# A one-core decoder trunk: last output piece of 128 columns instead of 256, and the first block's norm-weight product queued behind the third block's high part

## The chip, the cores and the metric

The kernel runs on one core of a Trainium2 chip. A core has TensorE (matrix products, PE in the profile), VectorE (DVE), ScalarE (ACT), GpSimd (POOL) and SyncE (SP). Each runs its own instructions in a fixed order, and they wait for one another through semaphores. SyncE, ScalarE and GpSimd also issue DMAs, which move data between the chip's main memory and the on-chip memory; the queue of the issuing engine is written SPq or ACTq. Products are gathered in PSUM, banks of 512 float32 per partition. The metric is the device time of one execution in microseconds (us). Three runs of the kernel before took 1330.47 to 1331.39 us, with a median of 1330.71 us.

## The reference

One layer of a decoder trunk on 1024 tokens with 1024 channels, in float32:

```python
xn = rmsnorm(x, norm_mix_w[l])
proj = xn @ w_in[l]
...
y_da = diff_attention(da_q, da_k, da_v, lam, lam_init, subln_w[l])
y_sw = sliding_window_attention(sw_q, sw_k, sw_v, sinks[l])
merged = jax.nn.sigmoid(g_da) * (y_da @ w_br_da[l]) + jax.nn.sigmoid(g_sw) * (y_sw @ w_br_sw[l])
x = x + merged @ w_mix_out[l]
xn = rmsnorm(x, norm_ffn_w[l])
x = x + conv_ffn(xn, w_up[l], conv_w[l], conv_b[l], w_down[l])
...
return rmsnorm(x, norm_final_w)
```

`rmsnorm` multiplies by 1/sqrt(mean of squares + eps) and by a weight per channel. Two places matter here: the input norm's weight with the first product, `xn @ w_in`, and the product with `w_down` with the final norm behind it.

## The kernel before

Everything is kept transposed: channels lie on the 128 partitions, in 8 blocks of 128 channels, and the 1024 tokens lie along the columns, in two halves of 512. Each float32 operand is split into a high part, rounded to the type that the profile calls fp32r, and a low part, the rest; a product is then three matmuls (high by high, high by low, low by high). In most of the products a scheme after Strassen and Winograd replaces eight block products by seven, at the price of sums and differences of blocks on VectorE and GpSimd.

The order in which each engine gets its instructions is worked out when the kernel is built: a planner simulates the engines and lets the instruction that is ready go first, by program order among the ready ones. `tc.issue_after(ins)` forbids part of that: what is written inside the block for the engine of `ins` is queued behind `ins`. It adds no wait for `ins` to finish, and other engines' instructions inside the block, such as a DMA issued by SyncE, are not held.

**The front** (`project`, L278 to L436). The blocks of x are loaded in the order 0, 4, 1, 5, 2, 6, 3, 7 (`rows`), the first two in halves. For each block `cut` (L348) writes the high part xh on ScalarE (L351, x times the norm weight, rounded) and the low part xl on VectorE (L352). `blocks` (L299) then issues the matmuls of this block for the three column blocks of `w_in` that are computed in the plain way (L304 to L306). Those weights come in pieces: the first block's, then three blocks' worth (`piece(n, 1, 4)`, L339 on ScalarE and L340 on VectorE). For the later products x itself is needed in differences: `scale(0)` (L370, L372) multiplies the blocks 0 and 4 by the norm weight on ScalarE, in place, `diffs(0)` (L312 to L315) makes four half differences on VectorE, and `parts(0)` (L838, L839) splits them. Only then are the buffers of the blocks 0 and 4 free for the blocks 3 and 7, since there are six. `square` (L364 to L368) collects the squares for the norm itself, which is applied after the product (L421, L429).

**The end** (`down`, L1078, and `last_norm`, L1234). The seven block products of `w_down` run as stages, the last of them "P4". Its four products m = 0 to 3 finish the first half's channel blocks 4 to 7. For m = 0 and 1 a product is 24 matmuls of 512 columns (L1169 in `product`). For m = 2 and 3 the 512 columns are cut into two pieces at `q` (L1093, 256 columns): first both products of columns 0 to 255, then both of columns 256 to 511. Behind each product come the eviction (L1223 on VectorE, x plus the PSUM sum), the square (L1158 on ScalarE), the sum of squares (L1160 on VectorE, not for the last channel block) and the product with the final norm's weight (L1161 on ScalarE).

`last_norm` gives back a list of steps for one piece of columns. `sums` adds the squares over the partitions with matmuls against ones (L185, one instruction stands twice for each block of 128 columns and operand), takes the mean on VectorE (L192) and the power -1/2 on GpSimd (L194). `spread` brings the result to all partitions with transposes (L200), twice, into two PSUM tiles, and copies the second one into the on-chip memory on ScalarE (L1251), because GpSimd's products read it there. Then come the scaled products of a few channel blocks each (L1259, on VectorE or GpSimd) with an output DMA for each (L1260), on SyncE and ScalarE in turn. For pieces shorter than 512 columns, `spread` and all products form one step. `tail` holds the steps that are still to be called: while the second piece's products are issued, `each` calls the first piece's steps, `sums` after the fifth k of m = 2 and the rest after the third k of m = 3. The second piece's steps are called behind everything.

## Time and profile before

| what | before |
|---|---|
| median of 3 runs | 1330.71 us |
| the profiled execution | 1330.42 us |
| its span, first to last instruction | 1328.4 us |
| granted TensorE clock, mean | 0.998 |
| VectorE, ScalarE, GpSimd busy | 1049.4, 614.7, 478.0 us |

The profiled execution lies 0.3 us below the median, and its span leaves out 2.0 us around the first and the last instruction. A row of the timeline has the start in us, the duration in us, the engine, the line, the operation, the tile written and those read, the shape, and how many such instructions follow one another (x2); in square brackets stands how long the engine was idle before and what released it. A row of the chain of waits has start, length and place of one link. A group's row has the busy time in us and the mean duration of one in ns. A row of the table by windows has the stretch, its length, the busy time and number of instructions of PE, PE's weight loads, DVE, ACT and POOL, the granted clock, the busy share of the DMA engines and GB/s. A row of the DMA issues has the queue, the count, the KB of one and the us from issue to landing.

### The profile page before, as it was taken

What the parts mean: (1) busy time and instruction counts of PE and PEld (TensorE: products, weight loads), DVE (VectorE), ACT (ScalarE), POOL (GpSimd) and SP (SyncE); (2) the same over time, 40 slices, a digit from 0 to 9 for tenths busy, and PEclk for the clock granted to TensorE, in tenths of its full rate; (3) what the DMA queues carried; (4) which work ended last, traced back from release to release, by engine and by line L of the source; (5) the groups of instructions that cost most, each with busy time, mean ns of one, the idle gap of its engine ahead of it and who ended that gap; (6) DMA issues with size and microseconds to landing.
All of it is one profiled execution on the core that took longest, in us unless ns stands there. A gap on an engine that the chain in (4) does not pass through costs nothing.

```text
span 1328.4 us, 17040 instructions
## 1 busy us (share of the span) xinstructions
PE 1315.8 (99%) x6264; PEld 1097.6 (83%) x6264; DVE 1049.4 (79%) x1431; ACT 614.7 (46%) x946; POOL 478.0 (36%) x364
## 2 busy tenths in 40 slices
PE   9999999999999999999999999999999999999997
PEld 7888888888888878888888888888888888888886
DVE  8846775289888976455669999999999997886654
ACT  9432232276667774333444443343434344345643
POOL 0446652001101015751435666665566631101111
PEclk9999999999999999999999999999999999999999
DMA  7334333966554236334422222122222228867532
GB/s 260 126 144 157 145 148 122 269 179 190 143 133 142 82 126 225 120 118 151 143 95 95 80 79 93 66 95 80 82 77 86 81 75 333 266 158 143 111 98 108
DMA packets 63234, 180.25 MB, mean 136 GB/s; under 512 B 6960, under 2 KB 16816, under 8 KB 63152
## 3 DMA queue, kind: packets, MB, share of 16 engines
q1 hardware_dynamic: 49120, 153.48, 35.1%
q0 software_dynamic: 2304, 8.39, 3.7%
q10 hardware_dynamic: 11728, 17.31, 3.6%
q8 instruction: 49, 0.80, 0.3%
q14 instruction: 33, 0.27, 0.1%
HBM read 130.39 MB, written 48.76 MB: 135 GB/s over the span
## 4 chain that ended last, share of the span: by engine, by line
PE 97%; ACT 1%; DVE 1%; DMA 0%; issue 0%; SPq 0%; POOLq 0%; POOL 0%; ACTq 0%
PE t L919 45%; PE y L1169 7%; PE d L1169 5%; PE g L177 4%; PE g L178 4%; PE g L179 4%; PE sc L177 3%; PE sc L179 3%; PE sc L178 3%; PE sc L651 3%; PE y L1120 2%; PE d L1120 2%; PE t L667 1%; PE t L770 1%; PE sc L739 1%; PE t L679 1%
## 5 line engine op out<-in xcount | busy, mean ns | idle before, releaser
L1063 POOL TENSOR_TENSOR us<-us,rstd 128x1024 f32<-128x1024 f32 x42 | 92.2, 2214 | 82.5 <-DVE us L484 47.6
L1072 ACT ACTIVATE c<-us,vecs 128x1024 f32<-128x1024 f32 x44 | 54.8, 1248 | 127.1 <-POOL us L1063 121.5
L137 DVE TENSOR_TENSOR sl<-sf,sh 128x1024 fp32r<-128x1024 f32 x62 | 89.3, 1441 | 12.8 <-ACT sh L135 12.8
L158 DVE TENSOR_TENSOR wl<-raw,wh 128x1024 fp32r<-128x1024 f32 (+1 forms) x49 | 68.0, 1389 | 35.5 <-ACT wh L156 25.9
L135 ACT CAST sh<-sf 128x1024 fp32r<-128x1024 f32 x62 | 64.6, 1044 | 62.1 <-PE t L919 44.0
L156 ACT CAST wh<-raw 128x1024 fp32r<-128x1024 f32 (+1 forms) x49 | 49.6, 1014 | 91.2 <-PE sc L178 33.4
L121 POOL TENSOR_TENSOR sf<-rv 128x512 f32<-128x512 f32 x30 | 50.4, 1679 | 99.5 <-DVE sl L137 59.0
L1169 PE MATMUL y<-h,wh 128*128 128x512 f32 (+1 forms) x288 | 80.8, 366 | 0.0
L1075 DVE SCALAR_TENSOR_TENSOR c<-us,vecs,c 128x1024 f32<-128x1024 f32 x44 | 78.5, 1817 | 0.0
L1074 DVE SCALAR_TENSOR_TENSOR c<-us,vecs,c 128x1024 f32<-128x1024 f32 x44 | 69.3, 1606 | 5.6 <-ACT c L1072 5.5
L123 POOL TENSOR_TENSOR sf<-raw,rv 128x512 f32<-128x512 f32 x30 | 56.7, 1890 | 46.6 <-DVE sl L137 46.6
L177 PE MATMUL g<-xh,wh 128*128 128x512 f32 x176 | 71.0, 404 | 1.5 <-ACT g L580 1.5
L178 PE MATMUL g<-xl,wh 128*128 128x512 f32 x176 | 70.3, 400 | 0.0
L179 PE MATMUL g<-xh,wl 128*128 128x512 f32 x176 | 70.2, 399 | 0.0
L1055 ACT ACTIVATE c<-c 128x1024 f32<-128x1024 f32 x22 | 23.4, 1063 | 83.4 <-DVE c L1075 83.4
L655 DVE CUSTOM_DVE_ANT_0 L<-sc,bias 128x128 f32<-128x128 f32 (+7 forms) x64 | 47.7, 752 | 17.0 <-PE sc L651 13.7
L634 POOL MEMSET aT<- 128x128 f32 x32 | 6.1, 204 | 151.8 <-PE t L680 98.0
L137 DVE TENSOR_TENSOR wl<-raw,wh 128x1024 fp32r<-128x1024 f32 (+1 forms) x32 | 59.7, 1864 | 0.1
L1169 PE MATMUL d<-h,wh 128*128 128x512 f32 x192 | 59.4, 390 | 0.0
L1169 PEld LDWEIGHTS y<-h,wh 128*128 128x128 f32 x288 | 52.1, 189 | 8.7
L122 POOL TENSOR_TENSOR sf<-sf,raw 128x512 f32<-128x512 f32 x31 | 58.2, 1878 | 2.2
L656 ACT ACTIVATE L<-L,sm 128x128 f32<-128x128 f32 (+7 forms) x64 | 49.6, 778 | 20.0 <-DVE sm L655 17.3
(411 smaller groups left out, 4255.4 us busy)
## 6 DMA issues: line engine op xcount, KB each, us to landing
u<-qd SPq DMA_DIRECT2D x72, 256.0 KB, 6.4
raw<-in_w_up SPq DMA_DIRECT2D x23, 512.0 KB, 3.5
raw<-in_w_in SPq DMA_DIRECT2D x22, 512.0 KB, 3.7
hd<-c SPq DMA_DIRECT2D x22, 512.0 KB, 2.6
rv<-in_w_up SPq DMA_DIRECT2D x21, 512.0 KB, 3.6
gr<-gd SPq DMA_DIRECT2D x16, 512.0 KB, 3.4
S<-in_w_down POOLq DMA_DIRECT2D x16, 512.0 KB, 6.7
qd<-us SPq DMA_DIRECT2D x15, 512.0 KB, 2.6
```

Of the source, the lines that this page charges most:

```text
L122: tt(sa[:, 1], sa[:, 0], g[:, 0], ALU.subtract)
L135: cast = nc.scalar.copy(hi, src)
L137: low = nc.vector.tensor_tensor(lo, src, hi.bitcast(F32), ALU.subtract)
L158: self.lo = (eng or nc.vector).tensor_tensor(wl, raw, wh.bitcast(F32), ALU.subtract)
L177: nc.tensor.matmul(ps, wh[:, kc + o, :], ah, start=first and n == 0, stop=False)
L178: nc.tensor.matmul(ps, wh[:, kc + o, :], al, start=False, stop=False)
L179: nc.tensor.matmul(ps, wl[:, kc + o, :], ah, start=False, stop=last and n == len(kcs) - 1)
L919: nc.tensor.matmul(ps, (ah, ah, al)[p][:, k, :], (bh, bl, bh)[p], start=first and n == p == 0, stop=last and p == 2 and n == len(ks) - 1, ...
L1063: i = (nc.vector if m % NF == 0 else nc.gpsimd).tensor_tensor(us[:, 2:], us[:, 2:], self.rstd, ALU.mult)
L1074: nc.vector.scalar_tensor_tensor(c, us[:, 1:T + 1], cw[1], c, ALU.mult, ALU.add)
L1075: nc.vector.scalar_tensor_tensor(c, us[:, 0:T], cw[0], c, ALU.mult, ALU.add)
L1169: nc.tensor.matmul(ps, v[:, k, :], x, start=start and k == i == 0, stop=k == 7 and i == 2, skip_group_check=True)
```

## The change

It has two parts.

At the front `cut` keeps its ScalarE instruction, and `third` is the one of the third block loaded, block 1. Both instructions of `scale(0)` are queued behind it on ScalarE.

At the end `q` becomes 384: the first piece has 384 columns, the last 128. The first piece's steps are now separate ones for all pieces: `sums` is called after the last k of m = 2 of the last piece, and three steps after the sixth k of m = 3: `spread`, the GpSimd product of channel blocks 6 and 7, and the VectorE product of blocks 0 and 1. The other two VectorE products, of blocks 2 and 3 and of blocks 4 and 5, are called among the last piece's own steps, the one ahead of its `sums`, the other ahead of its `spread`; on VectorE they are queued behind `ev`, the last eviction. The last piece's products are now of the channel blocks 0 to 2 (VectorE), 5 to 7 (GpSimd) and 3 and 4 (VectorE), three where there were four.

```diff
-                    nc.scalar.mul(self.xh[kc][:, a:b], x, wcol(kc))
+                    self.cut = nc.scalar.mul(self.xh[kc][:, a:b], x, wcol(kc))
...
                 for kc in rows[2:6]:
                     load(kc)
+                    if kc == rows[2]:
+                        third = self.cut.ins
                 nc.sync.dma_start(self.vecs[:, KC:], self.vecs_d[:, KC:])
                 for kc in rows[:2]:
                     square(kc)
-                scale(0)
+                with tc.issue_after(third):
+                    scale(0)
                 diffs(0)
...
-            q = H2 // 2
+            q = 3 * P
...
-                    product(ps, w, "P4", False, a, b, lambda k, m=m: tail.pop(0)() if a and k == (4 if m < 3 else 2) else None)
+                    def each(k, m=m):
+                        if a and m == 2 and k == 7:
+                            tail.pop(0)()
+                        if a and m == 3 and k == 5:
+                            for _ in range(3):
+                                tail.pop(0)()
+
+                    product(ps, w, "P4", False, a, b, each)
...
-                    tt(x, x, ps, ALU.add)
+                    ev = tt(x, x, ps, ALU.add)
...
-                tail = self.last_norm(psD, [acc[0][:, 0, a:b], sq], x3, 0, a, b, ((0, 1, nc.vector), (1, 3, nc.vector), (6, 8, nc.gpsimd), (3, 6, nc.vector)) if a else
-                                      ((0, 3, nc.gpsimd), (3, 5, nc.vector), (5, 8, nc.vector)))
+                last = self.last_norm(psD, [acc[0][:, 0, a:b], sq], x3, 0, a, b, ((0, 3, nc.vector), (5, 8, nc.gpsimd), (3, 5, nc.vector)) if a else
+                                      ((6, 8, nc.gpsimd), (0, 2, nc.vector), (2, 4, nc.vector), (4, 6, nc.vector)))
+                if a:
+                    def held(f):
+                        with tc.issue_after(ev.ins):
+                            f()
+
+                    last[1:1] = [lambda f=f: held(f) for f in tail[1:]]
+                    last[:0] = [lambda f=f: held(f) for f in tail[:1]]
+                tail = last
...
-        def rest():
-            spread()
-            for i in range(len(pieces)):
-                scale(i)
-
-        return [sums, rest] if b - a < H2 else [sums, spread] + [lambda i=i: scale(i) for i in range(len(pieces))]
+        return [sums, spread] + [lambda i=i: scale(i) for i in range(len(pieces))]
```

## The prediction

> **What bounds the kernel now.** I read the page first, then the chain of waits, then the timelines of both ends.

> ```profile
> span 1328.4 us, 17040 instructions
> ...
> PE 1315.8 (99%) x6264; PEld 1097.6 (83%) x6264; DVE 1049.4 (79%) x1431; ACT 614.7 (46%) x946; POOL 478.0 (36%) x364
> ...
> PE 97%; ACT 1%; DVE 1%; DMA 0%; issue 0%; SPq 0%; POOLq 0%; POOL 0%; ACTq 0%
> ```

> TensorE is busy 1315.8 of 1328.4 us and makes up 97% of the chain that ended last. All that anybody could take away besides its work is 12.6 us, and the change touches the two places where part of it sits: a wait near 14 us, and the stretch behind the last product. So each part of the change is priced by two questions: does TensorE issue more, and what happens in the places where it waits.

> **Part one, the front.** This is the timeline of ScalarE, one TensorE row, and the issues and the times to landing of two loads.

> ```profile
> 9.74 1.80 ACT L339 CAST wh<-raw 128x768 fp32r<-128x768 f32 x2 [0.41 <-DMA raw<-in_w_in]
> 11.45 1.15 ACT L372 ACTIVATE xr<-xr,vecs 128x1024 f32<-128x1024 f32 x1
> 12.50 0.82 ACT L339 CAST sh<-raw 128x768 fp32r<-128x768 f32 x1
> 13.23 1.14 ACT L351 ACTIVATE xh<-xr,vecs 128x1024 fp32r<-128x1024 f32 x1
> 14.27 1.14 ACT L372 ACTIVATE xr<-xr,vecs 128x1024 f32<-128x1024 f32 x1
> 15.31 1.14 ACT L351 ACTIVATE xh<-xr,vecs 128x1024 fp32r<-128x1024 f32 x1
> ...
> 14.42 1.20 PE L304 MATMUL t<-xh,wh 128*128 128x512 f32 x4 [0.66 <-ACT xh L351]
> ```

> ```profile
> 4.15 0.55 SPq L335 DMA_DIRECT2D raw<-in_w_in  x1
> 6.05 0.60 SPq L346 DMA_DIRECT2D xr<-in_xT  x1
> ...
> raw<-in_w_in SPq DMA_DIRECT2D x1, 384.0 KB, 5.6
> xr<-in_xT SPq DMA_DIRECT2D x1, 512.0 KB, 7.0
> ```

> L351 at 13.23 writes the high part of the third block of x; TensorE stands 0.66 us for it. Ahead of it on ScalarE stands L372 at 11.45, the first block's product. The change queues both L372 behind it. ScalarE's own work ahead would then end about 1.05 us earlier (12.50 - 11.45), more than the 0.66 us of the wait. But the block's load, issued at 6.05 as the first of its row, lands 7.0 us later, at 13.05. The other load shows how fast a landing is taken up: issued at 4.15, landed 5.6 later at 9.75, and L339 runs from 9.74. So L351 can start at about 13.05 instead of 13.23: **0.2 us** of the 0.66 are won, not all. The ends are 0.66 us won (if the load lands earlier than its rounded times say) and a loss.

> The loss would come through VectorE. L372 feeds the differences, which VectorE now makes from 12.63 on; they slide behind the third block's low part, and VectorE has nothing to put in their place.

> ```profile
> 20.00:40.00 20.00, 20.00 (x95) 16.72 (x93) 20.00 (x22) 18.47 (x19) 0.00 (x0) 1.00 0.29 102
> ...
> 42.83 1.22 DVE L839 TENSOR_TENSOR t13l<-xr,t13h 128x1024 fp32r<-128x1024 f32 x1
> 44.89 0.69 DVE L421 COPY rstd<-t 128x512 f32<-128x512 f32 x1 [0.84 <-PE t L200]
> ```

> In the table by windows VectorE (third busy column) is busy all of 20 to 40 us, so 0.6 us (one L312, 0.69 long) that slips stays slipped until 44.89, where VectorE stands 0.84 us for TensorE. That gap takes it up, so I cost it at nothing; without the gap it would cost those 0.6 us. The two loads that wait for the buffers of the first blocks slip with it and have more than that in hand. Front: -0.2 us, between -0.66 and +0.6.

> **Part two, TensorE in the last products.** The chain in order of time:

> ```profile
> 1184.36 21.76 PE d L1169 x96
> ...
> 1288.68 0.87 PE d L200 x8
> ...
> 1313.48 0.79 PE d L185 x8
> ...
> 1316.95 1.80 PE y L1169 x15
> ...
> 1318.78 0.43 DVE x L1223
> ...
> 1319.24 0.42 ACT c L1158
> ...
> 1319.71 0.84 PE d L185 x6
> ...
> 1320.57 0.17 DVE ms L192
> ...
> 1320.88 0.70 POOL rs L194
> ```

> A matmul of 512 columns takes 21.76/96 = 0.227 us, one of 256 takes 1.80/15 = 0.120. The line through both is 0.013 + 0.000417 per column: 384 columns 0.173, 128 columns 0.067. By that line 48 matmuls of 384 and 48 of 128 take just what 96 of 256 take, 11.5 us. But a matmul of few columns doesn't follow the line: L185 streams one column and takes 0.79/8 = 0.10 us, L200 streams 128 and takes 0.87/8 = 0.109. Each has its own 128x128 load of weights, as each L1169 has. I take 0.109, the row with 128 columns; the ends are 0.057 (a quarter of 0.227) and 0.120. Then the products take 48 x (0.173 + 0.109) = 13.5 us, **+2.0 us** (ends -0.5 and +2.5).

> The row for 128 columns is 0.109 us. [...]

> The first piece's sums and transposes, which sit between the products, grow with its blocks from two to three: L185 from 8 to 12 (+0.4), L200 from 4 to 6 (+0.2). Together TensorE reaches the end of its products **2.6 us later**. The new reciprocal root has three columns:

> ```profile
> 1283.36 1.99 POOL L194 TENSOR_TENSOR rs<-ms,mhalf 128x4 f32<-128x4 f32 x1 [34.99 <-DVE ms L192]
> ```

> It costs between 0.70 (two columns) and 1.99 (four). Sums to transposes are 18 matmuls, 2.0 us, and before the root go about 0.45 us; up to 1.5 us is hidden, so 0 to 0.5 us of stall; I take 0, since the two-column row is nearest in place.

> **Part three, behind the last product.** It ends at 1316.95 + 1.80 = 1318.75 now, and the rest is a chain of small steps, and of outputs:

> ```profile
> 1317.44 1.84 POOL L1259 TENSOR_TENSOR x<-x,rstd 128x768 f32<-128x768 f32 x1 [2.21 <-ACT rstd L1251]
> ...
> 1319.31 0.39 SPq L1260 DMA_DIRECT2D out_T<-x  x1
> ...
> 1322.10 1.89 DVE L1259 TENSOR_TENSOR x<-x,d 128x256 f32<-128x256 f32 x3 [1.36 <-PE d L200]
> 1322.32 0.37 ACT L1251 COPY rstd<-d 128x256 f32<-128x256 f32 x1 [2.12 <-PE d L200]
> 1322.77 1.27 POOL L1259 TENSOR_TENSOR x<-x,rstd 128x512 f32<-128x512 f32 x1 [1.19 <-ACT rstd L1251]
> ...
> 1324.02 0.45 ACTq L1260 DMA_DIRECT2D out_T<-x  x1
> ...
> L1259 DVE TENSOR_TENSOR x<-x,d 128x768 f32<-128x768 f32 x2 | 1.9, 949 | 0.0
> L1223 DVE TENSOR_TENSOR x<-x,y 128x256 f32<-128x256 f32 x4 | 1.7, 422 | 3.2 <-PE y L1169 3.2
> L1259 DVE TENSOR_TENSOR x<-x,d 128x512 f32<-128x512 f32 x2 | 1.4, 684 | 0.0
> ...
> out_T<-x ACTq DMA_DIRECT2D x1, 384.0 KB, 3.1
> ...
> out_T<-x SPq DMA_DIRECT2D x1, 128.0 KB, 1.8
> ...
> 1325.00:1326.50 1.50, 0.00 (x0) 0.00 (x0) 0.00 (x0) 0.00 (x0) 0.00 (x0) 0.50 1.08 384
> ...
> DMA packets 463, 0.22 MB, mean 318 GB/s; under 512 B 31, under 2 KB 462, under 8 KB 463
> ```

> The last landing now is 1324.02 + 3.1 = 1327.1, 8.4 us behind the last product, and 1.3 us of closing remain to 1328.4. I count the new steps from the end of the new last product. The eviction of 128 columns is 0.29 by the line through 0.422 and 0.684 (-0.13), the square about 0.1 shorter by the same slope, and behind it stand 2 instead of 6 sums (-0.44). The mean would be ready 1.3 us in (1320.74 - 1318.75 - 0.67), the root 0.15 later. Here something new stands in the way: the first piece's GpSimd product, 768 columns, 1.84 us, begins about when the last product ends, so the root waits until 1.8 (now 2.1). Then 0.70 for the root and 0.4 to the first scaled rows: 2.9 (now 3.35). The last GpSimd product has 384 columns, about 0.98 by the line through 1.27 and 1.84; its output goes out at about 4.3 instead of 5.3. VectorE's two held products (0.949 each) fit: one between eviction and mean, where VectorE waits for the sums (all but some 0.05 us), one while the root and the transposes run (1.1 us). Without that cover each would cost its 0.95.

> So the issue of the last output comes 1.0 us earlier in this count, and it is smaller. But the queue is fuller. Behind the last product go out three quarters of the 384-column piece, 3 x 393 KB, and 524 KB of the last one; now it is 2 x 393 KB and 1049 KB, the first of them already issued at 1319.31. On SP program order held in that row: the GpSimd piece went out at 1319.31 ahead of VectorE's, which was done at about 1318.3. So SP's first is out at 1.8, when GpSimd is done. A lone 128 KB output takes 1.8 us, of which 131 KB at 384 GB/s are 0.34, so 1.45 are fixed. Rows of 512 bytes I price at 318 GB/s, from a window of the start (3.7 to 4.4 us) whose packets have 476 bytes in the mean. 1.8 + 1.45 + 1.18 MB/384 GB/s (3.07) + 0.524 MB/318 GB/s (1.65) = 8.0 against 8.4: **-0.4 us**. If the issue alone decided, it would be 4.3 + 1.45 + 0.6 = 6.4, -2.0 us. If rows of 512 bytes are written at half of 318, +1.2.

> **Sum.** The profiled execution took 1330.42 us, 2.0 more than its span, 0.3 below the median of 1330.71. 1330.42 - 0.2 + 2.6 - 0.4 = 1332.4. I take 1332.4, which is +0.15%; about 0.2% (2.7 us) is what a measurement of this kernel can tell from no change.

> **The rivals.**

> 1. *128 columns go at the column rate.* Then the products add nothing, TensorE only the 0.6 of sums and transposes: 1330.42 - 0.2 + 0.6 - 0.4 = 1330.4. For it: 256 columns still lie near the line. Against it: both rows of few columns, 0.10 and 0.109. [...]
> 2. *The last issue decides, not the queue.* If SP sends the ready VectorE piece first, or the outputs overlap better than a plain sum of bytes, up to 2.0 us are won behind the product: 1330.42 - 0.2 + 2.6 - 2.0 = 1330.8. Against it: the table shows the DMA engines full (1.08) at the end already now.
> 3. *Slower than before by more than can be missed: short rows are slow to write.* The last piece's 512-byte rows in the output are written below about 225 GB/s; then 0.524 MB take 0.7 us more and the time passes 1333.1, and at half of 318 it is 1334.0. For it: no output in the trace has such short rows. Against it: loads of that size do 318. It decides only where the queue still ends last, and it passes the 2.7 us below about 200 GB/s.
> 4. *All at once: the front gives its whole 0.66 us,* with rivals 1 and 2 together 1330.42 - 0.66 + 0.6 - 2.0 = 1328.4, the lowest that the rows carry.

> **How the numbers follow.** Forecast 55%, rival 1 15%, rival 2 15%, rival 3 12%, rival 4 3%. The forecast's own range is 1331.4 to 1333.4 (front and root). With rivals 1 to 3 the range is 1329.5 to 1334.2. Faster by over 0.2% (below 1328.05) nobody but the last rival comes near: 3%. Slower by over 0.2% (above 1333.37) is rival 3 and the upper end of the forecast, with the root's stall or the front's loss: 17%. The rest, 80%, is within 0.2%.

> **What would show it.** In the changed kernel's front L351 of the third block should start near 13.05 with a wait of TensorE near 0.5; a start at 12.3 would make the landing wrong. The last 48 matmuls should be 0.109 apart; 0.067 makes the largest term wrong. The last root should start behind a GpSimd product of 1.84. The last output should land about 8.0 us behind the last product, with the DMA engines full from about 3 us on. A TensorE wait before the three pairs of transposes would show the root as too slow. If the middle of the kernel shows other waits than now, the new edge has moved more than its place.

## The result and the profile after

| | before | the change |
|---|---|---|
| median, range, runs | 1330.77 us, 1330.28 to 1331.39, 6 | 1340.32 us, 1339.57 to 1342.13, 6 |
| the profiled execution, its span | 1330.42 us, 1328.4 | 1340.33 us, 1338.3 |
| granted TensorE clock, mean | 0.998 | 0.993 |

The change makes the kernel slower, by a ratio of 1.0075 with a 95% interval of 1.0062 to 1.0088. The prediction of 1332.4 us is 7.9 us short and its range ended at 1334.2.

The page of the changed kernel, its span and busy times:

```profile
span 1338.3 us, 17041 instructions
...
PE 1322.5 (99%) x6264; PEld 1103.1 (82%) x6264; DVE 1053.0 (79%) x1431; ACT 614.4 (46%) x946; POOL 477.3 (36%) x364
```

TensorE has the same number of matmuls and is busy 6.7 us longer (1322.5 against 1315.8); the span has grown by 9.9. So there must be both a new wait and matmuls that take longer.

**Where the time went.** The chain of waits has the same rows far from both ends in both kernels, one right behind the front and one among the stages of the last seven products. First the kernel before, then the changed one:

```profile
64.27 171.36 PE t L919 x756
```

```profile
71.22 171.36 PE t L922 x756
...
1191.28 21.76 PE d L1172 x96
```

The second row started at 1184.36 before. So 6.9 us of the 9.9 are lost ahead of 1191 us, and all of that already ahead of 71 us, in the front; 3.0 are lost behind 1191 us.

**The front.** TensorE's waits by cause (total, times, longest), first the kernel before, then the changed one:

```profile
PE t L177 <- DVE xr L429: 0.3, 1, 0.3
```

```profile
PE t L177 <- DVE rstd L424: 5.1, 1, 5.1
```

A 5.1 us wait stands where 0.3 us stood. The table by windows of the changed kernel at that place (the first busy column is TensorE, the number behind the five engines is the granted clock):

```profile
50.00:52.00 2.00, 0.00 (x0) 0.00 (x0) 1.34 (x2) 2.00 (x3) 0.00 (x0) 0.52 0.00 0
52.00:54.00 2.00, 1.46 (x4) 1.17 (x5) 0.99 (x2) 1.47 (x2) 0.00 (x0) 0.50 0.00 0
54.00:56.00 2.00, 2.00 (x6) 1.61 (x5) 2.00 (x4) 0.00 (x0) 0.00 (x0) 0.50 0.00 0
56.00:58.00 2.00, 2.00 (x8) 1.55 (x8) 2.00 (x4) 0.78 (x1) 0.00 (x0) 0.77 0.03 8
58.00:60.00 2.00, 2.00 (x11) 1.63 (x10) 2.00 (x4) 0.28 (x1) 0.00 (x0) 1.00 0.47 193
```

The wait has a second price. While TensorE stands here, the granted clock falls from 1.00 to 0.50 (at 50.09, 2.7 us into the wait), and it stays there when TensorE is back: 6 matmuls run in the 2 us from 54, where 11 do at full clock (from 58). TensorE resumes at 52.54 and the clock is full again at 56.92 (0.77 over 56 to 58), so 4.4 us of work go at half speed, some 2.2 us. 4.8 more of waiting and 2.2 are 7.0, against the 6.9 of the shift. The second price is not the same in every execution: in the profiled one of `e1_front`, the front alone (below), the clock was 1.00 over 48 to 52, 0.58 over 52 to 56 and 1.00 from 56, so it was back at about 55.4, with TensorE at work again from 52.43, which makes some 1.5 us.

Who lets TensorE wait is in the timelines. Kernel before, ScalarE, VectorE and TensorE:

```profile
41.73 2.00 ACT L838 CAST t13h<-xr 128x1024 fp32r<-128x1024 f32 x2 [3.00 <-DVE xr L313]
48.15 1.06 ACT L135 CAST sh<-sf 128x1024 fp32r<-128x1024 f32 x1 [4.42 <-POOL sf L122]
...
46.91 1.27 DVE L429 TENSOR_TENSOR xr<-t,rstd 128x512 f32<-128x512 f32 x2
48.11 0.68 DVE L421 COPY rstd<-t 128x512 f32<-128x512 f32 x1
...
47.64 0.50 PE L177 MATMUL t<-xh,wh 128*128 128x512 f32 x1 [0.28 <-DVE xr L429]
```

The changed kernel:

```profile
48.64 1.04 ACT L135 CAST sh<-sf 128x1024 fp32r<-128x1024 f32 x1 [8.93 <-POOL sf L122]
49.59 1.04 ACT L841 CAST t13h<-xr 128x1024 fp32r<-128x1024 f32 x1
...
50.66 1.23 DVE L842 TENSOR_TENSOR t13l<-xr,t13h 128x1024 fp32r<-128x1024 f32 x1 [3.18 <-ACT t13h L841]
51.81 0.68 DVE L424 COPY rstd<-t 128x512 f32<-128x512 f32 x1
...
54.65 1.88 DVE L432 TENSOR_TENSOR xr<-t,rstd 128x512 f32<-128x512 f32 x3
...
52.54 0.79 PE L177 MATMUL t<-xh,wh 128*128 128x512 f32 x1 [5.13 <-DVE rstd L424]
```

Line numbers are 3 higher here. The cast of the first weight sum (L135) ends its wait for GpSimd at about the same time in both, 48.15 and 48.64. But before, the first high parts of block 2's and block 3's differences (both tiles are called `t13h`) stood ahead of it on ScalarE and were done at 43.7; now both stand behind it. The low part needs the high part, so it starts at 50.66 on VectorE.

Behind it on VectorE stand the two kinds of work that read a PSUM tile `t`, and by which the profile has TensorE released: the second copy of `rstd`, and the products of L432 (L429 before). Before, the products came first, at 46.91, and TensorE went on at 47.64, ahead of the copy, so that nothing waited for the copy. In the changed kernel the products come at 54.65, and the copy at 51.81 is the first of them; TensorE starts behind it, at 52.54.

Nobody edited these lines. The planner orders each queue anew, and in `e1_front` the edge at 14 us is all that was added; what in the planner's reckoning turned the two casts round is not shown.

What the front was to win did not come, since the third block's load sets the start. ScalarE and TensorE of the changed kernel:

```profile
13.22 1.15 ACT L351 ACTIVATE xh<-xr,vecs 128x1024 fp32r<-128x1024 f32 x1 [0.45 <-DMA xr<-in_xT]
...
14.43 1.20 PE L304 MATMUL t<-xh,wh 128*128 128x512 f32 x4
```

L351 now stands idle for the load, and starts at 13.22 against 13.23 before; TensorE goes on at 14.43 against 14.42 (its own wait there is nearly gone only because it had lost 0.6 us ahead of it: its last matmul there starts at 13.94, before at 13.38).

**The end.** The chain of waits of the changed kernel:

```profile
1301.96 21.86 PE y L1172 x120
...
1323.82 1.28 PE d L185 x12
...
1325.10 2.39 PE y L1172 x18
...
1327.49 1.30 PE d L200 x6
...
1328.79 1.19 PE y L1172 x6
```

The first link holds 48 matmuls of 512 columns, 48 of 384 and the first 24 of 128. The 128-column ones start 0.11 us apart, as the timeline of two stretches shows (a row's duration spans its overlapping matmuls; the starts count):

```profile
1321.03 0.33 PE L1172 MATMUL y<-h,wh 128*128 128x128 f32 x2
...
1323.54 0.28 PE L1172 MATMUL y<-h,wl 128*128 128x128 f32 x1
1323.65 1.44 PE L185 MATMUL d<-ones,c 128*128 128x1 f32 x12
```

24 of them take 1323.65 - 1321.03 = 2.62 us, 0.109 each. 21.86 - 48 x 0.227 - 2.62 leaves 8.34 for the 48 of 384, 0.174 each. That is the prediction's 0.109 and 0.173. But the second 24, the links of x18 and x6, take 3.58 instead of 2.62, and the six transposes 1.30. The table by windows says why:

```profile
1326.00:1327.00 1.00, 1.00 (x10) 1.00 (x10) 0.00 (x0) 0.00 (x0) 0.23 (x1) 0.84 0.00 0
1327.00:1328.00 1.00, 1.00 (x7) 1.00 (x7) 0.00 (x0) 0.00 (x0) 0.00 (x0) 0.50 0.00 0
```

The granted clock halves at 1326.68 (0.84 over that microsecond), with TensorE busy all the time by the profile. Before, no matmul of the last product was at half clock: it ended at 1318.75, and the table by windows of the kernel before has the full clock until at least 1322.

```profile
1320.00:1322.00 2.00, 0.91 (x8) 0.82 (x9) 0.16 (x1) 0.20 (x1) 0.70 (x1) 1.00 0.94 329
```

The last product ends at 1328.79 + 1.19 = 1329.98. Against 1318.75 + 6.92 that is 4.3 us later. Behind it, the last issue and what the DMA engines moved from 1329 to 1338.3 (40 equal slices):

```profile
1334.31 0.38 ACTq L1278 DMA_DIRECT2D out_T<-x  x1
...
GB/s 0 0 0 0 112 396 383 410 370 20 0 0 0 145 410 377 390 403 410 390 396 396 410 403 396 390 322 344 348 344 339 350 328 40 0 0 0 0 0 0
...
out_T<-x ACTq DMA_DIRECT2D x1, 192.0 KB, 2.8
```

The last output lands at 1334.31 + 2.8 = 1337.1, 7.1 us behind the last product, where it was 8.4: 1.3 us won. 4.3 - 1.3 = 3.0, the rest of the 9.9.

### The profile page after: what moved, and what is told of

The parts are those of the page before. It is cut to its first block, busy times and chain, and to the rows that moved or that the text cites. A ratio compares the mean times of both kernels' runs of the same rounds, so it can differ in the third digit from the quotient of the medians.

```text
span 1338.3 us, 17041 instructions
## 1 busy us (share of the span) xinstructions
PE 1322.5 (99%) x6264; PEld 1103.1 (82%) x6264; DVE 1053.0 (79%) x1431; ACT 614.4 (46%) x946; POOL 477.3 (36%) x364
## 4 chain that ended last, share of the span: by engine, by line
PE 96%; ACT 1%; DVE 1%; issue 1%; DMA 1%; POOL 0%; SPq 0%; POOLq 0%; ACTq 0%
PE t L922 44%; PE y L1172 7%; PE d L1172 5%; PE g L177 4%; PE g L178 4%; PE g L179 4%; PE sc L178 3%; PE sc L179 3%; PE sc L177 3%; PE sc L654 3%; PE y L1123 2%; PE d L1123 2%; PE t L670 1%; PE t L773 1%; PE sc L742 1%; PE t L682 1%
## 5 line engine op out<-in xcount | busy, mean ns | idle before, releaser
L135 ACT CAST sh<-sf 128x1024 fp32r<-128x1024 f32 x62 | 64.6, 1043 | 66.2 <-PE t L922 44.0
L121 POOL TENSOR_TENSOR sf<-rv 128x512 f32<-128x512 f32 x30 | 46.5, 1551 | 106.9 <-DVE sl L137 58.6
L1172 PE MATMUL y<-h,wh 128*128 128x512 f32 (+2 forms) x288 | 83.4, 373 | 0.0
L659 ACT ACTIVATE L<-L,sm 128x128 f32<-128x128 f32 (+7 forms) x64 | 49.6, 778 | 20.0 <-DVE sm L658 13.5
## 6 DMA issues: line engine op xcount, KB each, us to landing
raw<-in_w_up SPq DMA_DIRECT2D x23, 512.0 KB, 3.5
raw<-in_w_in SPq DMA_DIRECT2D x22, 512.0 KB, 3.9
hd<-c SPq DMA_DIRECT2D x22, 512.0 KB, 2.6
rv<-in_w_up SPq DMA_DIRECT2D x21, 512.0 KB, 3.5
gr<-gd SPq DMA_DIRECT2D x16, 512.0 KB, 3.4
S<-in_w_down POOLq DMA_DIRECT2D x16, 512.0 KB, 6.1
qd<-us SPq DMA_DIRECT2D x15, 512.0 KB, 2.6
```

What stands on the lines that cost most here:

```text
L135: cast = nc.scalar.copy(hi, src)
L1172: nc.tensor.matmul(ps, v[:, k, :], x, start=start and k == i == 0, stop=k == 7 and i == 2, skip_group_check=True)
```

## The experiments

Each time is the median, with its range; the kernel before on the same chip had 1331.37 us (1330.47 to 1333.29, 22 runs) beside e1 to e4, 1331.48 (1330.74 to 1332.58, 19) beside e5 to e8, and 1331.08 (1330.70 to 1332.14, 12) beside e9 and e10. A ratio is to these, with its 95% interval.

### The front alone, the end alone

`e1_front` is the kernel before with the two edits of the front (`self.cut`, `third`, `issue_after`) and nothing of the end; `e2_tail` has the edits of the end and not this one:

```diff
-                with tc.issue_after(third):
-                    scale(0)
+                scale(0)
```

> Only the front's part of the change (both products of scale(0) queued behind the third block's high part); the end is that of the kernel before. Theory A (queue order): the new edge makes the planner put ScalarE's cast of the first weight sum ahead of the high part that VectorE's second copy of rstd waits behind, so TensorE stands about 5 us near 47 to 52 us and then runs some 7 us at half clock: 1330.8 + 6.9 = 1337.7 us. Theory B (what I had priced): the front by itself is worth -0.2 to +0.6 us, and the large loss needs both parts together: 1330.6 to 1331.4 us.

> Only the end's part of the change (384 and 128 columns, the new order of the steps); scale(0) is not held. If the two parts add up, +3.0 us: 1333.8 us, with the last 48 products 0.11 us apart. Of the +3.0, my count has +2.2 (products +2.0, sums and transposes +0.6, outputs -0.4); the half clock from 1326.7 us on, seen in the changed kernel, would be the rest, and where the clock does not fall in these runs it is 1332.3 us.

The front alone took 1338.27 us (1337.77 to 1338.98, 4 runs), ratio 1.0053 (1.0037 to 1.0070); the end alone 1335.03 (1333.11 to 1337.94, 7 runs), ratio 1.0030 (1.0019 to 1.0041). 6.9 and 3.7 us are 10.6 together; the whole change cost 9.6, which the intervals allow. So the front holds two thirds of the loss, and neither part wins anything. TensorE's wait in e1_front is word for word the changed kernel's row, 5.1 us for `rstd` at L424, so the end has no part in it. e2_tail came out 1.2 us above its expectation of 1333.8. Its executions lie 4.8 us apart, and the three slowest have the lowest mean clock (0.994, the others 0.995 and 0.996).

### One edge more at the front, in two places

Both kernels keep the front's edit and leave the end as it was. `e3_front_mend` queues the preparation of the next weights, which holds the cast of L135, behind block 2's first high part on ScalarE, as it stood before:

```diff
             def parts(k):
                 for n, r in enumerate((k, k + 4)):
                     self.split(*ts[k][n], xr[r])
+                    if (k, n) == (2, 0):
+                        self.ahead_of_pair = self.high.ins
...
-                    with tc.issue_after(self.pow.ins), tc.high_priority(40):
+                    with tc.issue_after(self.pow.ins), tc.issue_after(self.ahead_of_pair), tc.high_priority(40):
...
-        self.nc.scalar.copy(hi, src)
+        self.high = self.nc.scalar.copy(hi, src)
```

`e5_copy_first` leaves ScalarE alone and moves the next link: on VectorE block 2's low parts are queued behind the second copy of `rstd`.

```diff
-                    nc.vector.tensor_copy(self.rstd[:, hf * H2:(hf + 1) * H2], ssq)
+                    copied = nc.vector.tensor_copy(self.rstd[:, hf * H2:(hf + 1) * H2], ssq)
...
-                    parts(k)
+                    with tc.issue_after(copied.ins) if k == 2 else nullcontext():
+                        parts(k)
```

> The front's part of the change, and one edge more: the next weights' casts on ScalarE (the first weight sums among them) are queued behind the high part of block 2's differences. The held products stay as late as in the change. Theory A: TensorE's wait of 5 us and the half clock behind it are gone: 1330.3 to 1331.0 us. Rival C (VectorE's differences, 3 us later than before, cost by themselves): a wait of over 2 us stays near 47 us, and the time is above 1333 us.

> The front's part of the change, and one edge more, on VectorE alone: the low parts of block 2's differences are queued behind the second copy of rstd. ScalarE's order is that of e1_front, with the cast of the weight sum still ahead of the high part. Theory A (TensorE waited for that copy, and the copy stood behind the low part): the wait of 5 us and the half clock are gone, 1331 to 1332.5 us. Rival D (the late high part itself is what TensorE needs next): the wait only moves to the next bank or operand, and the time stays above 1335 us.

e3_front_mend took 1332.01 us (1331.44 to 1332.77, 10 runs), ratio 1.0004 (0.9995 to 1.0013), and e5_copy_first 1332.04 (1331.44 to 1332.95, 10 runs), ratio 1.0003 (0.9994 to 1.0013). Either edge takes the loss away, to what cannot be told from the kernel before. In e5_copy_first the waits and timelines read:

```profile
PE t L177 <- DVE xr L432: 0.7, 1, 0.7
...
48.26 1.05 ACT L135 CAST sh<-sf 128x1024 fp32r<-128x1024 f32 x1 [8.94 <-POOL sf L122]
...
48.22 0.68 DVE L424 COPY rstd<-t 128x512 f32<-128x512 f32 x1
50.30 1.23 DVE L843 TENSOR_TENSOR t13l<-xr,t13h 128x1024 fp32r<-128x1024 f32 x1 [1.40 <-ACT t13h L842]
```

ScalarE still stands 8.9 us for GpSimd, and the low part is as late as in the changed kernel (50.30). It no longer matters, because VectorE's work that releases TensorE is ahead of it: the copy at 48.22 as before, and with it two products of L432 at 47.02, for which TensorE waits 0.7 us. So the link that costs is this work behind the low part. The one edge brought copy and products forward together, so the copy alone is not singled out.

### The order of the casts, forced on the kernel before

`e6_cast_ahead` is the kernel before, with `scale(0)` where it was; the first weight sum is prepared earlier in the program, and block 2's parts are queued behind its cast:

```diff
+                with tc.issue_after(self.pow.ins), tc.high_priority(40):
+                    four = self.sum_pair(next(s[0] for s in self.wsrc if s[1] == "pair"))
+                    self.early = four, self.split_pair(*four, 1, 2)
+                    scast = self.scast
...
-                    parts(k)
+                    with tc.issue_after(scast) if k == 2 else nullcontext():
+                        parts(k)
```

> The kernel before, with scale(0) where it was, but ScalarE's cast of the first weight sum put ahead of the high part of block 2's differences by hand (the first pair is loaded and its first sums split at an earlier place in the program, with the same work). Theory A (the order of these two casts costs, whatever brought it about): a wait of 4 to 6 us for the second copy of rstd and half clock behind it, 1337 to 1339 us. Rival C (it takes the late differences as well): less than 2 us, below 1333.4 us.

It took 1337.45 us (1336.80 to 1338.99, 4 runs), ratio 1.0048 (1.0033 to 1.0063). Its waits, windows and VectorE:

```profile
PE t L184 <- DVE rstd L428: 4.4, 1, 4.4
...
52.00:56.00 4.00, 4.00 (x10) 3.13 (x11) 4.00 (x6) 0.00 (x0) 2.60 (x2) 0.50 0.01 4
...
51.24 0.68 DVE L428 COPY rstd<-t 128x512 f32<-128x512 f32 x1
```

A wait almost as long and the same half clock, without the moved product, as its theory A had it (a wait of 4 to 6 us, 1337 to 1339 us). So the order of the casts is enough without the edge at 14 us. The kernel does a little more than turn two casts round: the weight sum is prepared earlier in the program, and its low part (at 48.87 on VectorE) also got ahead of the copy. That the held `scale(0)` costs no more than can be measured is what e3_front_mend and e5_copy_first show, which keep it.

### The end: pieces of 256, and fewer sums

`e4_tail256` is e2_tail with the old cut, so that the new order of the steps is left and the widths are as before. `e7_tail_third_sums` is e2_tail with the first piece's sums, mean and root for one of its three blocks of columns only; the other two blocks are scaled by that block's root.

```diff
-            q = 3 * P
+            q = H2 // 2
```

```diff
+            m = 1 if n == 3 else n
-            self.col_sums(ssq, sqs, n, 0)
-            box.append(self.rstd_cols(ssq, n, D))
+            self.col_sums(ssq, sqs, m, 0)
+            box.append(self.rstd_cols(ssq, m, D))
```

> The end's new order of steps and of scaled pieces, but pieces of 256 and 256 columns. If the shorter last piece is what costs, TensorE ends its products as in the kernel before and the clock stays full to the end of them: 1330.0 to 1331.2 us. If the new order of the steps costs (a root that comes too late for the transposes, held products in VectorE's way), it is above 1331.5 us and TensorE waits before the transposes.

> The end's part of the change, with the first piece's sums and root for its first block only; that block's values stand for the other two blocks, so two thirds of those sums are left out (4 instructions in place of 12, 0.9 us less on TensorE). Theory E (the 48 matmuls of 128 columns keep TensorE too thinly busy, so the clock falls): the clock still falls before the products end in most runs, and the runs still spread by over 2 us, around 1333.5 us. Rival F (the sums, with one column each, bring the clock down): full clock to the end of the products, 1332 us or less, and a spread like the kernel before's.

e4_tail256 took 1331.65 us (1330.77 to 1333.75, 10 runs), ratio 1.0001 (0.9992 to 1.0011): the order of the steps is worth nothing that can be told either way (the 1331.5 that its expectation names is passed, but the kernel before was 0.6 us above its earlier 1330.77 on this chip, and TensorE does not wait before the transposes), and the end's loss lies in the widths. e7_tail_third_sums took 1332.81 (1331.99 to 1335.36, 10 runs), ratio 1.0012 (1.0003 to 1.0022), 2.2 us less than e2_tail. The 8 sums left out are 0.85 us of work (8 x 1.28/12). The remaining 1.3 us are near the 1.6 that the half clock took in the changed kernel. The mean clock is 0.998 in each of the ten executions, which says that it held in all of them: the sign of rival F came, though not its 1332 or less. The end alone, then e7_tail_third_sums, by chain and window:

```profile
1320.86 1.30 PE d L200 x6
...
1320.00:1322.00 2.00, 2.00 (x12) 2.00 (x12) 0.44 (x1) 0.00 (x0) 0.00 (x0) 0.50 0.00 0
```

```profile
1320.27 0.69 PE d L200 x6
...
1320.00:1322.00 2.00, 1.73 (x17) 1.64 (x16) 1.35 (x3) 0.48 (x1) 0.47 (x1) 1.00 0.00 0
```

The same six transposes take 1.30 and 0.69 us, at clocks of 0.50 and 1.00. In the first TensorE was busy all of those 2 us. What was taken out of the second are eight matmuls that stream one column.

### The end with more work on TensorE

`e8_tail_fill` adds to e2_tail one matmul of 512 columns into a finished bank at each of the 16 steps of the last piece's two products; its result is not used. `e10_four_fills` has only four of them, at the first steps of the last product, right behind the sums:

```diff
+                        if a and m == 3 and k < 4:
+                            nc.tensor.matmul(chains[1][0], w[0][:, k, :], self.B["P4", k][0], start=True, stop=True, skip_group_check=True)
```

(e8_tail_fill has `if a:` alone.)

> The end's part of the change, with 16 matmuls of 512 columns more, one behind each k of the last piece's products, into a bank that is done with: 16 x 0.227 = 3.6 us of added work whose result nobody reads. Theory E: the clock stays full to the end of the products, so the whole is 1331.4 + 2.2 + 3.6 = 1337 us with little spread; against e2_tail's 1335.0 that is 1.5 us less than the added work. Without any part of the clock in it: 1335.0 + 3.6 = 1338.6 us, and the spread of e2_tail (4.8 us) stays.

> The end part alone, and four more matmuls of 512 columns, whose result is not used, right behind the first piece's sums of one column (the first four steps of the last product's chain): 4 x 0.283 = 1.1 us of work more than e2_tail. [...]

e8_tail_fill took 1336.85 us (1335.95 to 1338.29, 4 runs), ratio 1.0043 (1.0027 to 1.0060). Its chain and windows:

```profile
1324.35 0.67 PE d L200 x6
...
1324.00:1326.00 2.00, 2.00 (x17) 1.84 (x17) 1.06 (x2) 0.48 (x1) 0.40 (x1) 1.00 0.00 0
```

The clock is 1.00 in every window up to 1326, and 16 x 0.227 = 3.6 us of added work cost 1.8 us against e2_tail; theory E had 1337. The mean clock is 0.998 or 0.999 in each of the four executions. e10_four_fills took 1336.85 too (1336.69 to 1337.56, 4 runs), ratio 1.0043 (1.0028 to 1.0058), which is 1.8 us above e2_tail, for 4 x 0.227 = 0.9 us of added work. Its chain, TensorE's timeline and one window:

```profile
1317.43 1.44 PE L185 MATMUL d<-ones,c 128*128 128x1 f32 x12
...
1319.10 0.45 PE L1222 MATMUL y<-h,wh 128*128 128x512 f32 x1
...
1319.00:1320.00 1.00, 1.00 (x8) 0.95 (x8) 0.27 (x2) 0.00 (x0) 0.85 (x1) 0.85 0.00 0
```

The clock fell at 1319.7 all the same (0.85 over that microsecond, 0.50 in the next), when the first of the four fills, at 1319.10, was through and the second, at 1319.67, had just started. Shown is that with the sums cut to a third the clock was 1.00 in the window that has 0.50 in e2_tail (1320 to 1322), that with 16 wide matmuls it was 1.00 up to 1326, and that with four wide ones in this place it fell. Why it falls is not shown.

### The whole change with one edge

`e9_change_copy_first` is the changed kernel with the edit of e5_copy_first.

> The whole change, and on VectorE the low parts of block 2's differences queued behind the second copy of rstd, as in e5_copy_first. Theory (the front's loss is only the order of these two on VectorE, and the two ends add up): the first wait of TensorE near 48 us shrinks from 5.1 to 0.7 us, the granted clock stays full through the front, and the time is that of the end alone, 1335.0 (1333.5 to 1336.5), some 5 us below the change. Rival (part of the front's 7 us belongs to the two ends together, or to the moved product itself): over 1337.

It took 1334.46 us (1333.52 to 1336.42, 9 runs), ratio 1.0023 (1.0013 to 1.0033), 5.9 us below the change (6.2 when each is set against the kernel before on its own chip). TensorE's wait there is 0.7 us for `xr` at L432, as in e5_copy_first, and the clock is full:

```profile
52.00:56.00 4.00, 4.00 (x19) 3.31 (x18) 2.61 (x4) 1.45 (x3) 0.00 (x0) 1.00 0.00 0
```

19 matmuls in 4 us at full clock, and what is left is the loss of the end. No kernel tried was faster than the one before.

## Why the prediction was wrong, and where it was right

**The front: the step that failed.** The prediction bounded the front between -0.66 and +0.6, the upper end being VectorE's slip of 0.6 us, which it costed at nothing ("That gap takes it up"). The slip was about that size, 0.9 us by block 1's first low part (35.90 against 35.00 before); e3_front_mend and e5_copy_first keep a slip (36.01 and 35.48 there) and show no loss that can be told. What failed is the bound: the prediction took every queue's order as given and moved one instruction in it. But the order comes out of a planner that sorts all queues again: the cast of the weight sum went ahead of `t13h`, VectorE's copy of `rstd` and its products behind the low part, and TensorE waited 5.1 us and then worked 4.4 us at half clock, together 6.9 us where -0.2 was forecast. e6_cast_ahead shows that such an order costs it without the edge at 14 us, e5_copy_first and e9_change_copy_first that one edge brings it back. The last sentence of the prediction named the sign (other waits in the middle, if the edge had moved more than its place), but no rival priced it. Why the planner turned the two casts round was not followed further.

**The front's gain: right in its cause, zero in size.** The load sets the start, as predicted; it landed at 13.2, not at 13.05, so that nothing of the 0.2 us was left.

**The products, sums and transposes: right at full clock.** 0.109 and 0.174 us a matmul make 48 x 0.283 = 13.6 us against the forecast 13.5, and the sums grew by 1.28 - 0.79 = 0.5, the transposes (0.67 in e8_tail_fill) by 0.2. So rival 1, the column rate, did not happen. What sets the pace of 0.109 is not shown; at half clock it was 0.198 (1.19/6).

**The clock at the end: not in the prediction.** Every term was priced at full clock. The 24 last matmuls took 3.58 instead of 2.62 us and the transposes 1.30 instead of 0.67: 1.6 us, which no rival named. 4.3 us to the end of the products is the forecast's 2.6 and this. With eight of the twelve one-column sums left out (e7_tail_third_sums) the clock was 1.00 past the end of the products, up to 1324, and with 16 wide matmuls more (e8_tail_fill) up to 1326; why it fell without either is not shown.

**The root: right.** The root with three columns took 0.85 us, between the bounds, and TensorE did not stand for it.

**Behind the last product: 7.1 us, not 8.0.** The mechanism was right: SyncE's first output waits for GpSimd's product, and from then on the bytes fill the DMA engines to the end. GpSimd and SyncE in the changed kernel:

```profile
1329.38 1.81 POOL L1277 TENSOR_TENSOR x<-x,rstd 128x768 f32<-128x768 f32 x1 [3.15 <-ACT rstd L1269]
...
1331.22 3.04 SPq L1278 DMA_DIRECT2D out_T<-x  x4
```

The sizes were off, each a little. The half clock holds up the last products while GpSimd goes on, so its 1.81 us end 1.2 behind the last product, not 1.8 (in e7_tail_third_sums, at full clock, 1.7). By the row of GB/s above the 384-column piece is written at about 395 GB/s (384 was taken) and the 512-byte rows at about 340 (318), together 4.5 us instead of 4.7. What is left is 7.1 - 1.2 - 4.5 = 1.4 of fixed time, as forecast. So rival 3, slow short rows, did not occur; and rival 2's 2.0 us were not reached, as the DMA engines are busy without a gap from 1332.2 to 1336.7.

**The terms together.** Against the forecast the front is 7.1 us worse, the clock at the end 1.6 worse, the outputs 0.9 better, and the products, sums and transposes 0.1 worse: together the 7.9 us. The ranges would not have held the front's 6.9 in any case, but they were also not all worked out: by the bounds of front and root the forecast's own range is 1331.9 to 1333.7 and not 1331.4 to 1333.4, and for 1329.5 and 1334.2 the prediction shows no sum.

## What to carry to other kernels

Where a planner or scheduler sorts the queues, an ordering edge is not local: compare the order of every queue before and after, and look for an instruction that waits long and has newly got in front of something that was ready. A gain that is won by a narrower last piece must be set against what narrow matmuls cost, in their pace (here 0.109 us for 128 columns, where the line through 256 and 512 has 0.067) and in the clock (here 1.6 us at 0.50). A TensorE wait of some 5 us cost its length and another 1.5 to 2.2 us here, since the clock came back late.

## What the runs showed of the hardware

In the changed kernel the windows around both ends of the first half-clock stretch are:

```profile
50.00:50.50 0.50, 0.00 (x0) 0.00 (x0) 0.00 (x0) 0.50 (x1) 0.00 (x0) 0.59 0.00 0
...
56.50:57.00 0.50, 0.50 (x3) 0.37 (x2) 0.50 (x2) 0.00 (x0) 0.00 (x0) 0.58 0.14 33
```

0.59 in the first is 0.09 us at full clock, so the fall is at 50.09; 0.58 in the second puts the return at 56.92. So the half clock lasted 6.83 us; the next fall is at 1326.68. The same reckoning gives 3.4 us in e1_front (0.58 over 52 to 56, 1.00 on both sides) and 6.9 in e6_cast_ahead (0.83, 0.50 and 0.81 over the three stretches of 4 us from 48 to 60). What sets these lengths is not shown.

In four profiled executions it fell in the last product, 0.5 to 1.6 us behind the end of a dozen matmuls of one column among ones of 128: in the changed kernel at 1326.68, in e2_tail at 1320.0 (0.76 over 1319.5 to 1320.5), in e9_change_copy_first at 1320.5 (0.74 over 1320 to 1321) and in e10_four_fills at 1319.7. In three it was 1.00 past the sums: with four of one column up to 1324 (e7_tail_third_sums), with eight among ones of 256 up to 1324 (e4_tail256), and with a dozen and wide matmuls on both sides up to 1326 (e8_tail_fill). The last of these is the weakest: it is one profile, and only the mean clocks of the other three executions (0.998, 0.998 and 0.999) speak against luck.
